# Output projections of a two-layer decoder trunk: operand sums on VectorE, ScalarE and VectorE in a written order

## The chip, the core and the metric

One Trainium2 chip, of which the kernel uses one core. TensorE multiplies matrices, VectorE and GpSimd work element by element, ScalarE evaluates functions and copies, and the queue of SyncE issues all DMAs. The metric is the device time of one execution, in microseconds (us).

## What is computed

Two layers act on a residual stream `x` of 1024 tokens by 1024 features. Cut to what matters here:

```python
for layer in range(2):
    if layer == 0:
        ...                      # ya: gated linear recurrence, yb: sliding-window attention
        y = concat([ya * silu(ga), yb * silu(gb)])    # 1024 x 2048
        x = x + y @ w_out_a[0]                        # w_out_a: 2048 x 1024
    else:
        ...                      # h = rms_norm(x); u, v, g from h @ w_in_c; gated by chunks
        y = u * sg * silu(g)                          # 1024 x 2048
        x = x + y @ w_out_c[0]                        # w_out_c: 2048 x 1024
```

The change lies in the two products `y @ w_out`, the output projections. They are called projection A (layer 0) and projection C (layer 1) below.

## The kernel before

**Splitting.** Every float32 operand of a matrix product is split into a high part (a copy rounded to the fp32r type by ScalarE) and a low part (the difference, by VectorE). `mm3` (L144 to L147) makes a product of three matmuls: high times high, high times low, low times high. `split_a` (L685 to L689) splits a piece of the left operand into a tile named `wa`, `split_b` (L692 to L696) a piece of the right operand into tiles `wh_w` and `wl_w`. The low parts are thus L689 and L696 on VectorE, the high parts L688 and L695 on ScalarE. A piece is 128 x 1024 elements.

**Seven products for eight.** `winograd` (L706) makes a projection by quarters: both operands are cut into quarters, and seven products of sums of quarters take the place of eight. The contraction of 2048 is done as two halves, so there are 14 products, numbered 0 to 13 here (`turns`), and each contains 48 matmuls of 128 x 512: two operand pieces (its halves `j` = 0 and 1), four token tiles, two depths, three matmuls. Each needs a left operand (two `wa` pieces) and a right one (two `wh_w`/`wl_w` pieces). `wa3_0` is the left piece of product 3, half 0.

**The sums.** `sums_a` (L753) makes the sums of the left quarters (`s1` to `s4`): 16 operations of 128 x 1024 for each projection, on GpSimd through `combine` (L748). They are issued in front of products 1, 2, 3, 4, 5 and 7 (table `early`): 2, 4, 2, 4, 2 and 2 operations. The differences of the right quarters (`t1` to `t4`) are 16 more, on VectorE; `sources` issues both pieces of one (L748) ahead of the splitting of the first piece.

**Banks.** The products add up in two sets of four PSUM banks, one bank for each token tile. When the second half of the contraction is through, VectorE adds the four banks to the residual's rows `x1` (L824, called the eviction). It follows products 1, 3, 5, 8, 9, 11 and 13. Product 4 starts afresh in the four banks that products 2 and 3 filled, so its first matmul waits for the eviction after product 3. In projection A, `x1_done` then stores finished rows to `x1dram` and norms them for layer 1 (ScalarE squares with a sum, VectorE scales, GpSimd takes the power -0.5, VectorE multiplies); TensorE transposes normed rows during products 12 and 13.

**Buffers.** Quarters of `w_out` that are still to be used wait in four tiles (`braw`), loaded by SyncE's queue; a load waits until VectorE has read what was there. `wa` pieces have four tiles, `wh_w` and `wl_w` five each. `wa` of product s+1 can thus be written when product s-1 has been through the same half.

**Order.** A scheduler orders each engine's instructions, apart from engines under `manual_schedule`, which run in the order of the code. TensorE is under it throughout. The loop of `winograd` adds GpSimd and SyncE. ScalarE and VectorE are placed by the scheduler there. In the loop, the sums named in `early` for product s come first, then the operands of product s+1, then the matmuls of product s with their evictions. `sources` and `operands` start like this:

```python
            if i == 2:
                combine(nc.vector, t[n], b[n, "b12"], t[n], sub)
                return xs[n], t[n]
...
        def operands(s):
            load_b(s + 1)
            src_a, src_b = sources(*turns[s])
```

## Time and profile before

| | us |
|---|---|
| median of three runs | 1453.38 (1451.16 to 1453.53) |
| span of the profiled execution, first to last instruction | 1451.4 |
| TensorE busy | 1348.5 (93%) |
| VectorE busy | 1111.1 (77%) |
| ScalarE busy | 693.9 (48%) |
| GpSimd busy | 506.3 (35%) |
| chain that ended last, by engine | TensorE 59%, VectorE 22%, waiting for nothing that shows ("issue") 8%, GpSimd 4%, ScalarE 4%, DMA 3% |

The span is the time of one execution inside the profiler; the three runs were timed apart from it, and their median stands 2.0 us above the span. The page gives busy shares over the whole span, which mix stages with different limits, so the stages of the two projections (about 522 to 711 us and 1284 to 1448 us) have to be read from views of those stretches.

### The profile page before, as it was taken

To read this page: it belongs to the slowest core of one execution; us is meant where nothing else is said; L and a number is where in the kernel's file an instruction comes from. 1 tells how busy PE (TensorE), PEld (TensorE's weight loads), DVE (VectorE), ACT (ScalarE), POOL (GpSimd) and SP (SyncE) were. 2 spreads that over 40 slices of the span, in tenths; PEclk is the share of its full clock that TensorE was granted. 3 is DMA by queue.
4 is the path that set the end of the run, shared out by engine and by line. 5 is a ranking of instruction groups with operands and counts; after the bars stand their busy time and mean duration, and the time that the engine had idled before them with its cause. 6 is when DMAs were issued, how large, how long until landed. Compare 5 with 4: busy or idle time off the path is not lost.

```text
span 1451.4 us, 18932 instructions
## 1 busy us (share of the span) xinstructions
PE 1348.5 (93%) x7003; PEld 1148.9 (79%) x7003; DVE 1111.1 (77%) x1830; ACT 693.9 (48%) x1282; POOL 506.3 (35%) x350
## 2 busy tenths in 40 slices
PE   7999999999999996599998799999988998997998
PEld 6888888888887785488888799777777777775887
DVE  6468888888788889778678745778877887879873
ACT  6467878776777763134423223333333333432430
POOL 3322333221032339300035232444455444488100
PEclk9999999999999998799999899999999999999999
DMA  6212111112211054014412123233223322683321
GB/s 208 59 30 58 29 46 30 44 32 71 58 33 51 4 188 174 16 44 146 159 37 80 68 93 135 65 113 113 91 65 117 109 91 66 216 334 132 113 96 64
DMA packets 100536, 133.53 MB, mean 92 GB/s; under 512 B 5355, under 2 KB 72028, under 8 KB 98396
## 3 DMA queue, kind: packets, MB, share of 16 engines
q1 hardware_dynamic: 100444, 132.32, 27.1%
q8 instruction: 55, 0.90, 0.3%
q14 instruction: 37, 0.30, 0.1%
HBM read 107.11 MB, written 25.19 MB: 91 GB/s over the span
## 4 chain that ended last, share of the span: by engine, by line
PE 59%; DVE 22%; issue 8%; POOL 4%; ACT 4%; DMA 3%; SPq 0%; DVEq 0%; POOLq 0%; ACTq 0%
PE m L145 6%; PE m L146 5%; PE m L147 5%; DVE wlg L1142 3%; PE v L145 3%; PE v L146 3%; PE v L147 3%; DVE wl_w L696 2%; DVE wa L689 2%; PE pq L145 2%; PE gb L145 2%; PE pq L147 2%; PE gb L147 2%; PE pq L146 2%; PE gb L146 2%
## 5 line engine op out<-in xcount | busy, mean ns | idle before, releaser
L145 PE MATMUL m<-wh_w,wa 128*128 128x512 f32 x432 | 170.8, 395 | 34.0 <-DVE x L824 34.0
L146 PE MATMUL m<-wl_w,wa 128*128 128x512 f32 x432 | 170.5, 395 | 4.2 <-DVE wl_w L696 4.2
L147 PE MATMUL m<-wh_w,wa 128*128 128x512 f32 x432 | 170.0, 393 | 0.0
L145 PEld LDWEIGHTS m<-wh_w,wa 128*128 128x128 f32 x432 | 82.3, 190 | 52.9 <-issue 32.8
L146 PEld LDWEIGHTS m<-wl_w,wa 128*128 128x128 f32 x432 | 82.3, 190 | 21.6 <-DVE wl_w L696 5.0
L147 PEld LDWEIGHTS m<-wh_w,wa 128*128 128x128 f32 x432 | 82.3, 190 | 17.3
L1226 ACT CAST vh<-vg 128x256 fp32r<-128x256 f32 x64 | 26.0, 407 | 122.3 <-DVE vg L1224 122.3
L530 DVE CUSTOM_DVE_ANT_0 e<-ps,e,sink_bc 128x256 f32<-128x256 f32 (+1 forms) x128 | 62.3, 525 | 20.6 <-PE ps L527 20.2
L600 POOL TENSOR_TENSOR yb<-ot,yb 128x256 f32<-128x256 f32 x32 | 23.6, 736 | 144.9 <-DVE ot L598 127.2
L134 DVE TENSOR_TENSOR wl<-raw,wh 128x1024 fp32r<-128x1024 f32 x38 | 49.4, 1307 | 26.4 <-ACT wh L133 26.2
L1295 POOL TENSOR_TENSOR ug<-yt,ug 128x512 f32<-128x512 f32 x32 | 41.9, 1319 | 71.5 <-DVE yt L1294 71.4
L696 DVE TENSOR_TENSOR wl_w<-b,wh_w 128x1024 fp32r<-128x1024 f32 x36 | 60.7, 1693 | 6.8 <-ACT wh_w L695 6.8
L545 ACT ACTIVATE e<-e,nm 128x256 f32<-128x256 f32 (+1 forms) x128 | 61.6, 486 | 0.4 <-DVE nm L535 0.4
L695 ACT CAST wh_w<-b 128x1024 fp32r<-128x1024 f32 x36 | 37.5, 1046 | 46.9 <-DVE b L748 22.7
L1272 POOL TENSOR_TENSOR ug<-ug,sg 128x512 f32<-128x512 f32 x24 | 40.7, 1699 | 51.0 <-DVE ug L1271 51.0
L824 DVE TENSOR_TENSOR x<-m,x 128x512 f32<-128x512 f32 x56 | 37.4, 684 | 24.9 <-PE m L147 24.7
L902 POOL TENSOR_TENSOR ya<-ya,r 128x1024 f32<-128x1024 f32 x8 | 22.9, 2859 | 91.2 <-DVE r L898 65.5
L145 PE MATMUL pq<-hh,wh 128*128 128x512 f32 x128 | 52.5, 410 | 0.0
L145 PE MATMUL ga<-hh,wh 128*128 128x512 f32 x128 | 50.3, 393 | 2.2 <-DVE ya L867 2.2
L145 PE MATMUL gb<-hh,wh 128*128 128x512 f32 x128 | 50.3, 393 | 0.0
L145 PE MATMUL za<-hh,wh 128*128 128x512 f32 x128 | 50.2, 392 | 0.0
L147 PE MATMUL pq<-hh,wl 128*128 128x512 f32 x128 | 50.2, 392 | 0.0
(405 smaller groups left out, 4619.0 us busy)
## 6 DMA issues: line engine op xcount, KB each, us to landing
raw<-in_w_in_a_dram SPq DMA_DIRECT2D x34, 512.0 KB, 4.1
b<-in_w_out_a_dram SPq DMA_DIRECT2D x22, 512.0 KB, 6.9
b<-in_w_out_c_dram SPq DMA_DIRECT2D x22, 512.0 KB, 6.0
rawg<-in_w_in_c_dram SPq DMA_DIRECT2D x16, 512.0 KB, 3.6
rawu<-in_w_in_c_dram SPq DMA_DIRECT2D x16, 512.0 KB, 3.7
vg<-vdram SPq DMA_DIRECT2D x8, 1024.0 KB, 5.8
ydram<-ug SPq DMA_DIRECT2D x32, 256.0 KB, 2.4
yg<-ydram SPq DMA_DIRECT2D x8, 1024.0 KB, 10.8
```

Source lines behind the costliest of these rows:

```text
L134: nc.vector.tensor_tensor(out=lo, in0=raws[j], in1=hi.bitcast(F32), op=ALU.subtract)
L145: nc.tensor.matmul(acc, lhsT=lh, rhs=rh, start=first, stop=False, skip_group_check=shared)
L146: nc.tensor.matmul(acc, lhsT=lh, rhs=rl, start=False, stop=False, skip_group_check=shared)
L147: nc.tensor.matmul(acc, lhsT=ll, rhs=rh, start=False, stop=last, skip_group_check=shared)
L530: nc.vector.tensor_tensor_reduce(out=e[:, h, k0:256], in0=acc[:, j * 256:j * 256 + kw], in1=e[:, h, k0:256], scale=rs[:, 2 * (b % 4) + j:2 ...
L545: nc.scalar.activation(out=e[:, h], in_=e[:, h], func=AF.Exp, bias=st["nm"][:, h:h + 1], accum_out=st["sums"][:, h:h + 1])
L695: nc.scalar.copy(out=hi, in_=src)
L696: nc.vector.tensor_tensor(out=lo, in0=src, in1=hi.bitcast(F32), op=ALU.subtract)
L824: nc.vector.tensor_tensor(out=dst, in0=accs[m], in1=dst, op=add)
L1142: nc.vector.tensor_tensor(out=lo[:, j], in0=src, in1=hi[:, j].bitcast(F32), op=ALU.subtract)
L1272: nc.gpsimd.tensor_tensor(out=us[j], in0=us[j], in1=gates[j], op=ALU.mult)
L1295: nc.gpsimd.tensor_tensor(out=ug, in0=y.rearrange("p c t -> p (c t)"), in1=ug, op=ALU.mult)
```

## The change

In both projections:

- The 16 sums of the left operand run on VectorE.
- ScalarE and VectorE are also under `manual_schedule` in the loop, so they take their instructions in the order of the code.
- In the loop, the operands of product s+1 are issued first, then the sums that `early` names for product s, then the matmuls and evictions of product s.
- A difference of the right quarters is issued by halves: first piece of it, split of `wa` half 0, split of `w` half 0, then the second piece and half 1. Its line in the new file is L797.
- In projection A the norm of finished rows is cut into its steps, which are issued one and two token tiles later (`norms_step`), the last ones by `finish` after the loop.

The core of the diff:

```diff
+        def norms_step(least):
+        for one in norms:
+            one[0] += 1
+            if one[0] > least and len(one) > 1:
+                one.pop(1)()
...
             if i == 1:
-                combine(nc.gpsimd, xs[n], a21, a22, add)
+                combine(nc.vector, xs[n], a21, a22, add)
             elif i == 2:
-                combine(nc.gpsimd, a21, a11, a21, sub)
-                combine(nc.gpsimd, a11, xs[n], a11, sub)
+                combine(nc.vector, a21, a11, a21, sub)
+                combine(nc.vector, a11, xs[n], a11, sub)
             else:
-                combine(nc.gpsimd, a12, a12, a11, sub)
+                combine(nc.vector, a12, a12, a11, sub)
...
             if i == 2:
-                combine(nc.vector, t[n], b[n, "b12"], t[n], sub)
-                return xs[n], t[n]
+                return xs[n], t[n], (b[n, "b12"], t[n])
...
-            src_a, src_b = sources(*turns[s])
+            src_a, src_b, of = sources(*turns[s])
             pa, pb = [], []
             for j in range(2):
+                if of:
+                    nc.vector.tensor_tensor(out=src_b[j], in0=of[0][j], in1=of[1][j], op=sub)
...
-        manual = tc.manual_schedule(engines={ET.Pool, ET.SP})
+        manual = tc.manual_schedule(engines={ET.Activation, ET.DVE, ET.Pool, ET.SP})
...
+            nxt = operands(s + 1) if s + 1 < count else None
             for args in early.get(s, []):
                 sums_a(*args)
-            nxt = operands(s + 1) if s + 1 < count else None
...
+        finish()
         manual.__exit__(None, None, None)
...
-            _, rs = norm_rs(xt, f"c{t}", late["po"])
-            norm_mul(xt, xt, rs, late["gain_c"])
+            ss = norm_square(xt, f"c{t}", late["po"])[1]
+            rs = []
+            norms.append([0, lambda: rs.append(norm_root(ss, f"c{t}")),
+                          lambda: norm_mul(xt, xt, rs[0], late["gain_c"])])
```

The order of TensorE's instructions stays as it was, and SyncE's changes by one store in the norm's tail. In the rows below, `rawa0` is a right quarter that is turned into a difference in place, `b12_20_0` a quarter just loaded, `m2_0` the first of the four banks of products 2 and 3, and the last number of a name is a buffer's. First VectorE around the end of product 3 of projection A, before:

```order
L689 TENSOR_TENSOR wa4_1_5830<-sa0_1_5666,wa4_1_5830 128x1024
L696 TENSOR_TENSOR wl_w4_1_5834<-rawa1_5500,wh_w4_1_5833 128x1024
L748 TENSOR_TENSOR rawa0_5498<-b22_30_0_5893,rawa0_5498 128x1024
L696 TENSOR_TENSOR wl_w5_0_5903<-b11_0_5591,wh_w5_0_5902 128x1024
L748 TENSOR_TENSOR rawa1_5500<-b22_30_1_5895,rawa1_5500 128x1024
L689 TENSOR_TENSOR wa5_0_5899<-sa1_0_5813,wa5_0_5899 128x1024
L824 TENSOR_TENSOR x1_5570<-m2_0_5761,x1_5570 128x512
L696 TENSOR_TENSOR wl_w5_1_5910<-b11_1_5593,wh_w5_1_5909 128x1024
L824 TENSOR_TENSOR x1_5570<-m2_1_5762,x1_5570 128x512
```

and the same place now:

```order
L755 TENSOR_TENSOR yb0_472<-sa0_0_5683,yb0_472 128x2x512
L755 TENSOR_TENSOR yb1_1030<-sa0_1_5684,yb1_1030 128x2x512
L797 TENSOR_TENSOR rawa0_5498<-b12_20_0_5739,rawa0_5498 128x1024
L696 TENSOR_TENSOR wa4_0_5818<-sa0_0_5683,wa4_0_5818 128x1024
L703 TENSOR_TENSOR wl_w4_0_5822<-rawa0_5498,wh_w4_0_5821 128x1024
L797 TENSOR_TENSOR rawa1_5500<-b12_20_1_5741,rawa1_5500 128x1024
L696 TENSOR_TENSOR wa4_1_5826<-sa0_1_5684,wa4_1_5826 128x1024
L703 TENSOR_TENSOR wl_w4_1_5830<-rawa1_5500,wh_w4_1_5829 128x1024
L755 TENSOR_TENSOR sa1_0_5833<-ya0_4518,ya2_5091 128x1024
L755 TENSOR_TENSOR sa1_1_5834<-ya1_4754,ya3_5453 128x1024
L830 TENSOR_TENSOR x1_5570<-m2_0_5761,x1_5570 128x512
L830 TENSOR_TENSOR x1_5570<-m2_1_5762,x1_5570 128x512
```

Work on the operands of products 5 and 6 stood ahead of the eviction of `m2_0`; now only the operands of product 4 and two sums do, and sums stand among the operands.

Second, VectorE in the last spatial products of layer 1, just before projection C. `yt` adds the banks `s7`, which projection C's first product takes over; `first_c`, `wa0` and `wl_w0` are operands of product 0, `wa1` and `wl_w1` of product 1. Before:

```order
L1271 TENSOR_TENSOR ug7_3_11283<-u7_0_11284,ug7_3_11283 128x512
L696 TENSOR_TENSOR wl_w1_0_11537<-b11c_11493,wh_w1_0_11536 128x1024
L1271 TENSOR_TENSOR ug7_1_11281<-u7_2_11286,ug7_1_11281 128x512
L689 TENSOR_TENSOR wa0_1_11518<-yg1_11488,wa0_1_11518 128x1024
L696 TENSOR_TENSOR wl_w1_1_11544<-b11c_11493,wh_w1_1_11543 128x1024
L1268 TENSOR_TENSOR ug7_2_11282<-u7_0_11284,sg7_11076 128x512
L689 TENSOR_TENSOR wa1_0_11533<-yg4_11496,wa1_0_11533 128x1024
L1292 TENSOR_TENSOR yt7_0_0_11415<-s7_0_0_0_11416,sb7_11070 128x256
L1292 TENSOR_TENSOR yt7_0_0_11415<-s7_0_0_1_11421,sb7_11070 128x256
L689 TENSOR_TENSOR wa1_1_11540<-yg5_11498,wa1_1_11540 128x1024
L1294 TENSOR_TENSOR yt7_0_0_11415<-s7_0_0_0_11416,yt7_0_0_11415 128x256
```

and now:

```order
L696 TENSOR_TENSOR wa0_1_11518<-yg1_11488,wa0_1_11518 128x1024
L1290 TENSOR_TENSOR ug7_1_11281<-u7_2_11286,ug7_1_11281 128x512
L703 TENSOR_TENSOR wl_w0_1_11522<-rawc1_11486,wh_w0_1_11521 128x1024
L696 TENSOR_TENSOR wa1_0_11533<-yg4_11496,wa1_0_11533 128x1024
L1287 TENSOR_TENSOR ug7_2_11282<-u7_0_11284,sg7_11076 128x512
L703 TENSOR_TENSOR wl_w1_0_11537<-b11c_11493,wh_w1_0_11536 128x1024
L1311 TENSOR_TENSOR yt7_0_0_11415<-s7_0_0_0_11416,sb7_11070 128x256
L1311 TENSOR_TENSOR yt7_0_0_11415<-s7_0_0_1_11421,sb7_11070 128x256
L696 TENSOR_TENSOR wa1_1_11540<-yg5_11498,wa1_1_11540 128x1024
L703 TENSOR_TENSOR wl_w1_1_11544<-b11c_11493,wh_w1_1_11543 128x1024
L1313 TENSOR_TENSOR yt7_0_0_11415<-s7_0_0_0_11416,yt7_0_0_11415 128x256
```

`wl_w0_1`, which stood some 25 instructions earlier, now stands between `wa0_1` and the first sum that frees a bank (before, at L1294), and `wa0_1` comes ahead of the `wl_w1` pieces instead of between them.

Third, GpSimd from the end of mixer A on, before:

```order
L902 TENSOR_TENSOR ya3_5453<-ya3_5453,r7_5466 128x1024
L748 TENSOR_TENSOR sa0_0_5665<-yb0_472,yb2_1826 128x1024
L748 TENSOR_TENSOR sa0_1_5666<-yb1_1030,yb3_2677 128x1024
L748 TENSOR_TENSOR yb0_472<-yb0_472 128x2x512
L748 TENSOR_TENSOR yb1_1030<-yb1_1030 128x2x512
L748 TENSOR_TENSOR yb0_472<-sa0_0_5665,yb0_472 128x2x512
```

and now:

```order
L900 TENSOR_TENSOR it7_5467<-it7_5467,xa7_5354 128x1024
L909 TENSOR_TENSOR ya3_5453<-ya3_5453,r7_5466 128x1024
L163 TENSOR_TENSOR nrsc0_6305<-nmc0_6306,half_neg_81 128x1
L163 TENSOR_TENSOR nrsc1_6321<-nmc1_6322,half_neg_81 128x1
L163 TENSOR_TENSOR nrsc2_6337<-nmc2_6338,half_neg_81 128x1
```

The 16 sums between `ya3` and the powers of the norm are gone from it.

## Rows read from the trace of the kernel before

**Rows 1.** TensorE's waits, 521 to 712 us: us in total, times, longest.

```profile
PE m L145 <- DVE x L824: 24.6, 1, 24.6
PE m L146 <- DVE wl_w L696: 4.2, 2, 2.2
```

**Rows 2.** TensorE's waits, 1277 to 1448 us.

```profile
PE m L145 <- DVE x L824: 9.4, 3, 7.4
PE m L145 <- DVE yt L1294: 2.3, 1, 2.3
```

**Rows 3.** Timeline of TensorE, projection A: start us, us, instruction, [idle before <-releaser].

```profile
521.87 0.41 PE L145 MATMUL m<-wh_w,first_a 128*128 128x512 f32 x1
...
546.18 0.50 PE L146 MATMUL m<-wl_w,wa 128*128 128x512 f32 x1 [2.00 <-DVE wl_w L696]
...
559.53 0.79 PE L146 MATMUL m<-wl_w,wa 128*128 128x512 f32 x1 [2.17 <-DVE wl_w L696]
...
596.61 0.76 PE L145 MATMUL m<-wh_w,wa 128*128 128x512 f32 x1 [24.59 <-DVE x L824]
...
693.69 1.04 PE L196 MATMUL ptc<-ident,x 128*128 128x128 f32 x8
...
710.89 0.39 PE L145 MATMUL v<-wh,gh 128*128 128x512 f32 x1
```

**Rows 4.** Timeline of TensorE, projection C; 34 matmul starts after 1439.69.

```profile
1283.64 0.47 PE L145 MATMUL m<-wh_w,first_c 128*128 128x512 f32 x1 [2.33 <-DVE yt L1294]
...
1439.69 0.39 PE L146 MATMUL m<-wl_w,wa 128*128 128x512 f32 x1
...
1447.40 0.39 PE L147 MATMUL m<-wh_w,wa 128*128 128x512 f32 x1
```

**Rows 5.** Stretches: us, each engine's busy us (count), granted clock, DMA share, GB/s.

```profile
571.90:596.60 24.70, 0.12 (x1) 0.02 (x1) 24.70 (x10) 3.04 (x3) 22.88 (x7) 0.59 0.14 51
596.60:603.00 6.40, 6.39 (x20) 5.17 (x21) 6.40 (x8) 0.00 (x0) 0.00 (x0) 0.70 0.01 3
```

**Rows 6.** Timeline of VectorE, projection A, 564 to 596 us.

```profile
564.98 1.21 DVE L748 TENSOR_TENSOR rawa<-b,rawa 128x1024 f32<-128x1024 f32 x1
566.11 3.42 DVE L748 TENSOR_TENSOR b<-b,b 128x1024 f32<-128x1024 f32 x1
569.46 3.43 DVE L696 TENSOR_TENSOR wl_w<-rawa,wh_w 128x1024 fp32r<-128x1024 f32 x1
...
595.78 0.68 DVE L824 TENSOR_TENSOR x<-m,x 128x512 f32<-128x512 f32 x1
```

**Rows 7.** Timeline of GpSimd in the same stretch.

```profile
558.35 3.35 POOL L748 TENSOR_TENSOR sa<-ya,ya 128x1024 f32<-128x1024 f32 x1
565.20 3.25 POOL L748 TENSOR_TENSOR sa<-ya,ya 128x1024 f32<-128x1024 f32 x1 [3.50 <-DVE wa L689]
...
588.18 6.60 POOL L748 TENSOR_TENSOR ya<-ya,ya 128x1024 f32<-128x1024 f32 x2
```

**Rows 8.** A group of VectorE, 620 to 712 us: xcount, busy us, mean ns, idle before.

```profile
L696 DVE TENSOR_TENSOR wl_w<-b,wh_w 128x1024 fp32r<-128x1024 f32 x11 | 13.3, 1219 | 0.4 <-ACT wh_w L695 0.4
```

**Rows 9.** Timeline of ScalarE: two casts of projection A, two of C.

```profile
548.45 1.05 ACT L695 CAST wh_w<-b 128x1024 fp32r<-128x1024 f32 x1 [3.35 <-DMA b<-in_w_out_a_dram]
549.76 1.05 ACT L695 CAST wh_w<-b 128x1024 fp32r<-128x1024 f32 x1 [0.27 <-DMA b<-in_w_out_a_dram]
...
1274.56 1.06 ACT L688 CAST wa<-yg 128x1024 fp32r<-128x1024 f32 x1 [0.74 <-PE u L146]
...
1308.51 1.05 ACT L688 CAST wa<-yg 128x1024 fp32r<-128x1024 f32 x1 [2.81 <-DMA yg<-ydram]
```

**Rows 10.** Timeline of VectorE just before projection C.

```profile
1262.93 2.14 DVE L696 TENSOR_TENSOR wl_w<-rawc,wh_w 128x1024 fp32r<-128x1024 f32 x1
...
1283.08 0.74 DVE L1294 TENSOR_TENSOR yt<-s,yt 128x256 f32<-128x256 f32 x2
```

**Rows 11.** DMA issues, whole span: count, KB each, median us from issue to landing.

```profile
b<-in_w_out_a_dram SPq DMA_DIRECT2D x22, 512.0 KB, 6.9
```

More of the change, by code (lines that the diff above doesn't have):

```diff
@@ L172, in norm_rs, with norm_root @@
         nc.scalar.activation(out=xs, in_=xt, func=AF.Square, accum_out=ss)
+        return xs, ss
+    def norm_root(ss, t):
         rs = small.tile([P, 1], F32, tag="nrs", name=f"nrs{t}")
         power_rsqrt(rs, (ss, 1.0 / D), 1, f"nm{t}")
-        return xs, rs
+        return rs
+    def norm_rs(xt, t, pool):
+        xs, ss = norm_square(xt, t, pool)
+        return xs, norm_root(ss, t)
     def norm_mul(xt, xs, rs, gain, parts=1):
@@ L707, in raw_quarter, with winograd @@
         return load_quarter(lambda j: rawpool.tile([P, 2, 512], F32, tag="raw", name=f"{name}{j}"), w, r0, nh)
-    def winograd(acc_tiles, pool_of, w, parts, b11, first_a, done, after):
+    def winograd(acc_tiles, pool_of, w, parts, b11, first_a, done, after, finish):
         sub, add = ALU.subtract, ALU.add
@@ L769, in sources @@
             if i == 0:
-                return quarter(n, 0, 0), b11[n]
+                return quarter(n, 0, 0), b11[n], None
             if i == 1:
-                return quarter(n, 1, 0), b[n, "b21"]
+                return quarter(n, 1, 0), b[n, "b21"], None
             if i == 2:
-                combine(nc.vector, t[n], b[n, "b12"], t[n], sub)
-                return xs[n], t[n]
+                return xs[n], t[n], (b[n, "b12"], t[n])
             if i == 3:
-                combine(nc.vector, t[n], b[n, "b22"], t[n], sub)
-                return quarter(n, 0, 0), t[n]
+                return quarter(n, 0, 0), t[n], (b[n, "b22"], t[n])
             if i == 4:
-                return quarter(n, 1, 0), b[n, "b22"]
+                return quarter(n, 1, 0), b[n, "b22"], None
             if i == 5:
-                combine(nc.vector, b[n, "b11"], t[n], b[n, "b11"], sub)
-                return quarter(n, 0, 1), b[n, "b11"]
-            combine(nc.vector, t[n], b[n, "b21"], t[n], sub)
-            return quarter(n, 1, 1), t[n]
+                return quarter(n, 0, 1), b[n, "b11"], (t[n], b[n, "b11"])
+            return quarter(n, 1, 1), t[n], (b[n, "b21"], t[n])
         def operands(s):
             load_b(s + 1)
-            src_a, src_b = sources(*turns[s])
+            src_a, src_b, of = sources(*turns[s])
             pa, pb = [], []
             for j in range(2):
+                if of:
+                    nc.vector.tensor_tensor(out=src_b[j], in0=of[0][j], in1=of[1][j], op=sub)
                 if s == 0 and j == 0:
@@ L981, in x1_done @@
             nc.sync.dma_start(out=x1dram[t * P:(t + 1) * P, :], in_=xt)
-            _, rs = norm_rs(xt, f"c{t}", late["po"])
-            norm_mul(xt, xt, rs, late["gain_c"])
+            ss = norm_square(xt, f"c{t}", late["po"])[1]
+            rs = []
+            norms.append([0, lambda: rs.append(norm_root(ss, f"c{t}")),
+                          lambda: norm_mul(xt, xt, rs[0], late["gain_c"])])
+    norms = []
+    def norms_step(least):
[3 more added lines that the diff above has]
+                one.pop(1)()
     def out_a_after(s, j, m):
+        norms_step(1)
         if s == 0 and j == 0 and m == 0:
@@ L1000, in trunk_kernel @@
     winograd(x1, lambda: late["po"], w_out_a, [(1024, yb.__getitem__), (0, ya.__getitem__)], b11, first, x1_done,
-             out_a_after)
+             out_a_after, lambda: [norms_step(0) for _ in range(2)])
     last_spec[0] = len(specs) - 1
@@ L1355, in out_c_after @@
             load_x1(x1dram, x2)
-    winograd(x2, lambda: sp, w_out_c, [(0, yg.__getitem__), (1024, lambda g: yg[4 + g])], b11, first, store, out_c_after)
+    winograd(x2, lambda: sp, w_out_c, [(0, yg.__getitem__), (1024, lambda g: yg[4 + g])], b11, first, store, out_c_after,
+             lambda: None)
 def distance_onehot():
```

2 lines of the change are left out of this document (1 added, 1 removed).

## The prediction

> **What bounds the kernel now.** I read TensorE's waits in the two stretches of the projections first, then its timeline there, and then what VectorE and GpSimd did while it waited. TensorE is busy 93% of the span, so a gain can only come from the places where it stands or runs slowly.
>
> Projection A begins at 521.87 and the next stage's first matmul at 710.89 [rows 3]: 189.0 us. What it has to do: matmuls in an unbroken run start 7.71 / 34 = 0.227 us apart [rows 4], so a product of 48 takes 10.9 us and 14 take 152.4; four groups of transposes of about 1.04 us (one of them stands in [rows 3]) bring it to 156.5. So 32.5 us are lost. Waits are 24.6 + 4.2 = 28.8 of them [rows 1], and the remaining 3.7 are the clock: the matmul after the 2.17 us wait takes 0.79 instead of 0.39, and from 596.6 to 603.0 the granted clock averages 0.70, which alone costs 0.30 x 6.4 = 1.9 [rows 3, 5]. Projection C runs from 1283.64 to 1447.40 + 0.23 [rows 4]: 164.0 against 152.4, so 11.6 lost, of which 9.4 are waits for the eviction [rows 2] and 2.2 the clock after them. Both together: 44.1 us. The last wait each time is the eviction, VectorE's L824.
>
> Why is VectorE late? From 571.9 to 596.6 it is busy the whole 24.7 us with ten instructions, and GpSimd 22.9 us with seven [rows 5]. The same operation takes 1.21 us at 564.98 and 3.42 at 566.11 [rows 6]. Between the two, at 565.20, GpSimd starts again after 3.50 us of rest [rows 7]. GpSimd's own sums take 3.3 us, and an eviction, which reads one operand from PSUM, stays at 0.68 [rows 6, 7]. After 620 us, with GpSimd almost quiet, the low parts average 1.22 us [rows 8]. Back to back they start 1.14 apart (564.98 to 566.11 [rows 6]), since 0.08 overlaps. So a sum on GpSimd stretches each VectorE operation beside it by about 2.2 us, and the low parts, differences and the eviction behind them pile up until TensorE stands.
>
> **The change part by part.**
>
> *Sums moved.* 16 for each projection leave GpSimd and cost VectorE 16 x 1.14 = 18.2 us. The operations that were stretched come back to 1.14. What VectorE now has to do for a product is: four low parts, in most products two differences, zero to four sums, and an eviction of four (4 x 0.6 back to back) after some. With "during product s" for what is queued while TensorE does product s: during product 2, 4 low parts + 4 sums = 8 x 1.14 = 9.1; during 3, 6 + 2 sums + eviction = 8 x 1.14 + 2.4 = 11.5; during 4, 6 + 4 sums = 11.4; during 5, 11.5; during 7, 8 x 1.14 = 9.1; the others 4.6 to 9.3, with norms about 12 around product 10. Against 10.9 that is 1.7 us too much over products 3 to 5 and then slack. Operands are needed only at the end of the product, so this much is covered by being early; the exception is the eviction ahead of product 4.
>
> *Where the queue stands at product 4 of A.* Product 0 starts at 521.87 as before, so product 4 can start at 521.9 + 4 x 10.9 = 565.5. VectorE now keeps the written order: eviction after product 1, operands of 3, four sums, operands of 4, two sums, eviction after 3. The operands of product 3 wait for a load: ScalarE's cast starts at 548.45 when the data land [rows 9]. I allow 0.5 later, since the last step of mixer A on VectorE comes one low part later and the loads queue behind it. Then: cast until 550.0, low part until 551.2, two more (the second cast follows at 549.76 [rows 9]) until 553.4, four sums until 558.0, operands of 4 with 6 x 1.14 + 0.2 (the cast of each half has to come between a difference and its low part, which leaves about 0.1 a half) until 565.0, two sums until 567.3, first bank evicted at 568.0. TensorE waits 2.5 us at product 4. Bounds: 0 if the load lands as much earlier, 6 if it lands 3.5 us later. A wait of 2.17 was followed by the slow clock, one of 2.00 and one of 2.33 were not [rows 3, 4]; at about half a chance of 1.6 us I add 0.8. Products 5 to 13 then find their operands ready: the eviction ends at 569.7, operands of 5 at 576.8, TensorE needs them at 578.9. A loses 3.3 us instead of 32.5.
>
> *Loads and buffers.* The loads need 6.9 us from issue to landing [rows 11]; each has more than a product (10.9 us) between the low part that frees its buffer and the difference that reads it, so in-order waiting on them costs nothing except at product 3, counted above. If that cover were gone, each late load would stop VectorE and the eviction queued behind it. SyncE's loads are issued in the same order. ScalarE needs four casts of about 1.0 us in 10.9: nothing. The norm's steps go behind evictions and run while products 10 to 13 are multiplied; the rows are not transposed until 693.69 [rows 3], some 14 us later than their finished banks: nothing, and at most 1 us if a store must land before a row may be overwritten.
>
> *The start of C.* `wl_w0_1`, done at 1262.93 for 2.14 us beside GpSimd [rows 10], now comes after `wa0_1`, whose cast starts at 1274.56 when TensorE frees its tile [rows 9]; it stands ahead of the sum at 1283.08 [rows 10], which frees the bank that product 0 waits for at 1283.64 [rows 4]. So product 0 starts later by 1.1 to 2.1, less what VectorE has gained by then because those 2.14 us are gone from 1262.93. I take 0.5, and 0.9 for the chance that TensorE, standing longer there, gets the slow clock: 1.4 together, bounds -1 and +4.
>
> *Product 4 of C.* The last left quarter of product 3 is cast at 1308.51 [rows 9], then by the same steps: low parts until 1311.9, four sums 1316.5, operands of 4 at 1323.5, two sums 1325.8, first bank 1326.5. TensorE gets there at 1283.6 + 0.3 + 4 x 10.9 = 1327.5, and the start's delay moves both. I take 0.3, bounds 0 and 3.
>
> *Sum.* 44.1 - 3.3 - 1.4 - 0.3 = 39.1 us. Against the profiled execution: 1451.4 - 39.1 = 1412.3. The median of the runs stands 2.0 above that span, so I forecast 1453.4 - 39.1 = 1414.3.
>
> The sum goes against a rule, so I weigh it. VectorE is 100% busy exactly where the end is set [rows 5], and the change gives it 32 more operations. The Trainium skill (Perfetto Trace Analysis, Optimizing Scalar/DVE Operations) says that when VectorE is saturated, offloading to ScalarE or even GpSimd may make sense. By that rule alone the change goes the wrong way; the sum by it is the 1489.9 of rival 3. The same section warns that the two engines share a read port, so that moving work between them might not help; the 1.21 against 3.42 us is what decides here.
>
> **The rivals.**
>
> 1. *VectorE becomes the bound in products 3 to 5.* If the written order lets nothing overlap, an operation costs 1.23 (its full length and a little) instead of 1.14: 8 x 1.23 + 2.8 = 12.6, 12.3 and 12.6 against 10.9 make 4.8 more at each projection, and each then has a few us at the slow clock. A loses 3.3 + 4.8 + 2.6 = 10.7, C 1.4 + 4.8 + 1.3 = 7.5: 1453.4 - 44.1 + 18.2 = 1427.5. For it: the margin is thin. Against it: back-to-back rows start 1.14 apart wherever GpSimd rests.
> 2. *The start of C takes back its gain.* The last spatial sums wait behind the operands at full stretch beside GpSimd: 4 instead of 1.4, and 3 at product 4 instead of 0.3: 1414.3 + 5.3 = 1419.6.
> 3. *Slower: VectorE stays as full as it is.* If the stretch came from the place (these tiles, or loads that land there) and not from GpSimd, the 32 sums would come on top: at 1.14 each 1453.4 + 36.5 = 1489.9, and stretched to 3.4 like their neighbours still more (products 2 to 5 hold 34 operations and two evictions of 2.4 against 4 x 10.9 = 43.6 us of matmuls, so 34 x 3.4 + 4.8 - 43.6 = 77 us in each projection: 1453.4 - 44.1 + 154 = 1563). It decides from (43.6 + 22 - 4.8) / 34 = 1.79 us for an operation: there a projection loses the 22 us that it loses now on average. Against it: the jump from 1.21 to 3.42 comes within one microsecond of GpSimd's start, on the same line and shape, and the operations before it ran in the same place. The rule of the Trainium skill named above would give this case's lower time.
> 4. *Better: no new wait.* Both new waits and the clock losses vanish and C starts 1 us earlier: 1453.4 - 45.1 = 1408.3.
>
> **How the numbers follow.** The forecast has 0.70, rival 1 has 0.13, rival 2 has 0.09, rival 3 has 0.03, rival 4 has 0.05. The range goes from 1407 (rival 4 with 1 us to spare) to 1426, which takes in rival 2 and the bounds of product 4 (6 and 3) and of the start (+4) together, 1414.3 + 8.8 = 1423.1, and the nearer part of rival 1. About 0.2%, 2.9 us, is what a measurement can tell here. All cases but the third are faster by far more than that; between them and the third lies little, so faster 0.96, same 0.01, slower 0.03.
>
> **What would show it.** Right: VectorE's 128 x 1024 operations in both projections at 1.21 to 1.23 throughout, sums included; GpSimd idle from the end of mixer A to the first norm; the wait for the eviction at product 4 down from 24.6 and 7.4 to a few us; projection A some 160 us long, C some 153. Wrong: 3 us operations with GpSimd idle (rival 3); waits of TensorE for low parts at products 5 to 7 (rival 1); a wait for `yt` at the start of C of 5 us or more (rival 2); a VectorE that stands idle for loads while TensorE waits for it, which I have priced at nothing after product 3.

## The result and the profile after

| | before | after |
|---|---|---|
| median of the runs, us | 1453.45 (1451.16 to 1454.42, four runs) | 1415.03 (1414.49 to 1415.83, four runs) |
| span of the profiled execution, us | 1451.4 | 1412.7 |
| projection A, first matmul to the next stage's first, us | 189.0 | 160.1 |
| from there to projection C's first matmul, us | 572.8 | 574.0 |
| projection C, first to last matmul, us | 164.0 | 155.0 |

The ratio is 0.9744 (95% interval 0.9731 to 0.9758), 38.4 us less. The page of the changed kernel (busy time, share of the span, instructions):

```profile
PE 1346.6 (95%) x7003; PEld 1150.1 (81%) x7003; DVE 1094.0 (77%) x1862; ACT 693.7 (49%) x1282; POOL 399.3 (28%) x318
```

VectorE has 32 operations more and is busy 17 us less; GpSimd is busy 107 us less. TensorE's waits of the changed kernel from 515 to 690 us (first line) and the longest from 1230 to 1412 us (second), which answer to [rows 1, 2]:

```profile
PE m L145 <- DVE x L830: 2.1, 1, 2.1
...
PE m L145 <- DVE yt L1313: 3.8, 1, 3.8
```

The wait of 24.6 us is down to 2.1, the waits inside projection C are gone, and the one at its start has grown from 2.3 to 3.8. TensorE's timeline, as in [rows 3, 4]:

```profile
519.89 0.40 PE L145 MATMUL m<-wh_w,first_a 128*128 128x512 f32 x1
...
565.85 0.47 PE L145 MATMUL m<-wh_w,wa 128*128 128x512 f32 x1 [2.11 <-DVE x L830]
...
679.99 0.39 PE L145 MATMUL v<-wh,gh 128*128 128x512 f32 x1
...
1253.95 0.76 PE L145 MATMUL m<-wh_w,first_c 128*128 128x512 f32 x1 [3.75 <-DVE yt L1313]
...
1408.71 0.39 PE L147 MATMUL m<-wh_w,wa 128*128 128x512 f32 x1
```

VectorE's timeline at the place of [rows 6], and GpSimd's only instruction between 520 and 630 us:

```profile
555.78 1.22 DVE L797 TENSOR_TENSOR rawa<-b,rawa 128x1024 f32<-128x1024 f32 x1
...
562.75 2.35 DVE L755 TENSOR_TENSOR sa<-ya,ya 128x1024 f32<-128x1024 f32 x2
565.02 2.47 DVE L830 TENSOR_TENSOR x<-m,x 128x512 f32<-128x512 f32 x4
567.41 1.21 DVE L797 TENSOR_TENSOR b<-b,b 128x1024 f32<-128x1024 f32 x1
```

```profile
534.34 3.34 POOL L909 TENSOR_TENSOR ya<-ya,r 128x1024 f32<-128x1024 f32 x1 [14.35 <-DVE ya L874]
```

The difference `b<-b,b`, which took 3.42 us, takes 1.21, and the sums, now on VectorE, take 2.35 for two. One stretched operation is left in projection A, beside that last product on GpSimd:

```profile
535.33 3.44 DVE L703 TENSOR_TENSOR wl_w<-b,wh_w 128x1024 fp32r<-128x1024 f32 x1
```

### The profile page after: what moved, and what is told of

The parts are those of the page before. It is cut to its first block, busy times and chain, and to the rows that moved or that the text cites. A ratio compares the mean times of both kernels' runs of the same rounds, so it can differ in the third digit from the quotient of the medians.

```text
span 1412.7 us, 18904 instructions
## 1 busy us (share of the span) xinstructions
PE 1346.6 (95%) x7003; PEld 1150.1 (81%) x7003; DVE 1094.0 (77%) x1862; ACT 693.7 (49%) x1282; POOL 399.3 (28%) x318
## 4 chain that ended last, share of the span: by engine, by line
PE 68%; DVE 16%; issue 6%; POOL 5%; ACT 3%; DMA 2%; SPq 0%; DVEq 0%; POOLq 0%; ACTq 0%
PE m L145 6%; PE m L147 6%; PE m L146 6%; DVE wlg L1161 3%; PE v L145 3%; PE v L147 3%; PE v L146 3%; PE pq L145 2%; PE gb L145 2%; PE pq L147 2%; PE gb L147 2%; PE pq L146 2%; PE gb L146 2%; PE ppt L572 2%; DVE vg L1243 2%
## 5 line engine op out<-in xcount | busy, mean ns | idle before, releaser
L703 DVE TENSOR_TENSOR wl_w<-b,wh_w 128x1024 fp32r<-128x1024 f32 x36 | 46.2, 1284 | 7.8 <-ACT wh_w L702 7.6
L147 PE MATMUL gb<-hh,wl 128*128 128x512 f32 x128 | 49.9, 390 | 0.0
```

The lines of the kernel that those rows point to most:

```text
L147: nc.tensor.matmul(acc, lhsT=ll, rhs=rh, start=False, stop=last, skip_group_check=shared)
L703: nc.vector.tensor_tensor(out=lo, in0=src, in1=hi.bitcast(F32), op=ALU.subtract)
```

## Experiments

All ratios are to the kernel before on the same chip.

### The two halves of the change apart

```diff
 kernel before:                                    # engine alone
-                combine(nc.gpsimd, xs[n], a21, a22, add)      (and the three like it)
+                combine(nc.vector, xs[n], a21, a22, add)
 changed kernel:                                   # order alone
-                combine(nc.vector, xs[n], a21, a22, add)      (and the three like it)
+                combine(nc.gpsimd, xs[n], a21, a22, add)
```

> The kernel before with one edit: the 16 sums of each projection are issued to VectorE; the scheduler still places ScalarE and VectorE, sums stand ahead of the next operands, differences are issued in pairs, norms whole. Theory G (a sum on GpSimd stretches each VectorE operation beside it from 1.14 to about 3.4 us): the stretch goes with the engine alone, so most of the gain is here. VectorE's 128 x 1024 operations in both projections are at 1.2; the wait for the eviction at product 4 of A falls from 24.6 to some 3 to 10 us, since operands of products 5 and 6 (4 to 6 operations of 1.14) may still stand ahead of it; total about 1420, from 1414 to 1430. Rival O (the written order is what pays, the engine is second): the operands ahead of the eviction keep most of the wait, 1440 or more.

Measured: 1420.88 us, ratio 0.9784 (0.9768 to 0.9800). TensorE's waits from 515 to 715 us, and VectorE's timeline ahead of the first of them:

```profile
PE m L146 <- DVE wl_w L696: 5.4, 1, 5.4
PE m L145 <- DVE x L824: 2.2, 2, 1.2
```

```profile
547.14 1.22 DVE L748 TENSOR_TENSOR yb<-sa,yb 128x1024 f32<-128x1024 f32 x1
548.27 1.22 DVE L696 TENSOR_TENSOR wl_w<-b,wh_w 128x1024 fp32r<-128x1024 f32 x1
```

The stretch went with the engine, and the total came out as the first theory had it. But the wait that is left is at another place than expected: the scheduler put seven sums ahead of an operand of product 2, so TensorE waited 5.4 us there, and only 2.2, in two waits, for the eviction.

> The changed kernel with one edit: the 16 sums of each projection go back to GpSimd; written order, differences by halves and norms by steps stay. Theory G: VectorE has 22 operations in products 2 to 5 (22 x 1.14 + two evictions of 2.4 = 29.9 us) and 12 sums on GpSimd beside them stretch some 12 of them by 2.2: 56.3 us against 43.6 of matmuls, so about 12.7 us are lost in each projection, with the slow clock after it some 3: 1415 + 31 - 4 (losses that it replaces) = 1442, from 1428 to 1465; 128 x 1024 operations of VectorE at 3.4 us in both. Rival O: the written order keeps the evictions in time, 1415 to 1422.

Measured: 1428.64 us, ratio 0.9842 (0.9827 to 0.9856). The wait for the eviction in A, and VectorE around it, with GpSimd beside it:

```profile
PE m L145 <- DVE x L830: 8.6, 1, 8.6
```

```profile
568.71 3.37 DVE L696 TENSOR_TENSOR wa<-sa,wa 128x1024 fp32r<-128x1024 f32 x1
572.00 3.36 DVE L703 TENSOR_TENSOR wl_w<-rawa,wh_w 128x1024 fp32r<-128x1024 f32 x1
575.28 2.47 DVE L830 TENSOR_TENSOR x<-m,x 128x512 f32<-128x512 f32 x4
```

```profile
567.66 6.62 POOL L755 TENSOR_TENSOR ya<-ya 128x1024 f32<-128x1024 f32 x2
```

The stretch is back, as in [rows 6]. Yet the time is 13 us under the estimate, at the lower end of its range, and 24 us under the kernel before. In written order the eviction runs right behind the operands of product 4, where in the kernel before it stood behind work on products 5 and 6. A wait of 24.6 becomes 8.6 by that alone: with the sums still on GpSimd, 16 of the 24.6 us were the order (six operations of products 5 and 6 stood ahead of the eviction, at some 3.3 us each, of which not all showed as wait). Lost time in projection A (its length less the 156.5 of work): 32.5 before, 14.3 with the order alone, 10.6 with the engine alone, 3.6 with both. In C: 11.6, 6.8, 1.6, 2.6. **Each half gives most of the gain by itself, and the gains overlap**: 31.4 us for the engine alone and 23.7 for the order alone (1452.3, the kernel before on that chip, less 1420.9 and 1428.6), 38.4 together. Once the engine is changed, the order thus adds some 7 us and not 23.7. Neither rival holds in its pure form.

### GpSimd kept busy beside the moved sums

Three kernels add work to the changed one in `winograd`'s loop, into a scratch tile that nothing reads, each by one of the three statements in the inner loop:

```diff
             for args in early.get(s, []):
                 sums_a(*args)
+                for x in range(4 if args[1] != 2 else 8):
+                    wh = nxt[1][x // 2 % 2][0].bitcast(F32)[:, x % 2, :]
+                    nc.gpsimd.tensor_tensor(out=scratch, in0=wh, in1=wh, op=add)     # kept busy
+                    nc.gpsimd.tensor_scalar(out=scratch, in0=wh, scalar1=1.0,        # one input
+                                            scalar2=None, op0=add)
+                    nc.gpsimd.memset(scratch, 0.0)                                   # writes only
```

> The changed kernel with work added that computes nothing of the result: where a pair of sums is issued on VectorE, GpSimd also adds pieces of the high parts just cast to themselves, into a scratch tile that nobody reads (128 x 512, 64 of them in each projection, 1.30 us each where nothing runs beside them, so as many bytes as the sums had). VectorE has the same instructions on the same tiles. Theory G: VectorE's 128 x 1024 operations beside them go from 1.21 to about 3.4 us; the 24 pieces that fall to products 2 to 5 are worth 12 sums, 12 x 2.2 = 26 us on a VectorE that has 43.6 us of work there against 43.6 of matmuls; with the clock 1415 + 2 x 26 = 1467, from 1440 to 1485. Rival P (the stretch comes from the place, the tiles or the loads that land there): VectorE stays at 1.21 and the total at 1415.

> The changed kernel with work added that computes nothing of the result: the same 64 pieces of 128 x 512 in each projection as with GpSimd kept busy (1444.2 measured), but each adds a constant to the piece, so it reads one operand from SBUF where that one read two. If a VectorE operation with two operands in SBUF and a GpSimd operation that reads SBUF take turns as wholes (2.06 for a VectorE operation between pieces of 1.98 there, 3.4 between sums of 3.3), it makes no difference how many operands GpSimd reads: VectorE's operations beside the pieces last 1.14 plus the piece's own time, and the total lies between 1430 and 1460. If GpSimd's second operand is what costs, VectorE stays at 1.21 and the total at 1415.

> The changed kernel with work added that computes nothing of the result: in the places of the 64 pieces GpSimd fills the scratch tile with zeros, so it reads nothing from SBUF; with nothing to wait for, these run in a row from the end of mixer A on, and from the last spatial product on. If only GpSimd's reading makes the two take turns, VectorE's operations beside the fills stay at 1.21 and the total at 1415, within 1.5. If anything that GpSimd does in SBUF makes them take turns, operations beside the fills are longer by a fill each, and 16 to 32 of them in products 0 to 3 of each projection make the evictions late: 1425 or more.

Measured: 1444.23 us (ratio 0.9948, 0.9933 to 0.9963), 1427.50 us (0.9838, 0.9818 to 0.9858) and 1416.88 us (0.9765, 0.9745 to 0.9784). Each projection has 32 pieces (the last row below), 64 in both; the first two expectations give 64 to each. VectorE and GpSimd in the three, in this order, at the same operands:

```profile
553.50 2.06 DVE L703 TENSOR_TENSOR wl_w<-b,wh_w 128x1024 fp32r<-128x1024 f32 x1
555.48 4.03 DVE L755 TENSOR_TENSOR yb<-yb 128x1024 f32<-128x1024 f32 x2
```

```profile
550.48 15.87 POOL L818 TENSOR_TENSOR scratch<-wh_w 128x512 f32<-128x512 f32 x8 [4.99 <-ACT wh_w L702]
```

```profile
554.02 1.65 DVE L703 TENSOR_TENSOR wl_w<-b,wh_w 128x1024 fp32r<-128x1024 f32 x1
555.59 3.23 DVE L755 TENSOR_TENSOR yb<-yb 128x1024 f32<-128x1024 f32 x2
```

```profile
551.44 16.62 POOL L818 TENSOR_SCALAR scratch<-wh_w 128x512 f32<-128x512 f32 x10 [6.65 <-ACT wh_w L702]
```

```profile
552.86 1.22 DVE L703 TENSOR_TENSOR wl_w<-b,wh_w 128x1024 fp32r<-128x1024 f32 x1
554.00 2.35 DVE L755 TENSOR_TENSOR yb<-yb 128x1024 f32<-128x1024 f32 x2
```

```profile
538.09 18.66 POOL L818 MEMSET scratch<- 128x512 f32 x32
```

Same instructions of VectorE, same tiles, same place: 1.22 us beside fills, 1.65 beside pieces that read one operand, 2.06 beside pieces that read two, and 3.4 beside the sums of twice their size [rows 6]. So the cause is GpSimd, and what counts is that it reads SBUF; the place is out. Beside the eight pieces of the first kernel's row eight operations of VectorE are stretched, and ten beside the ten of the second, so the two engines take turns. VectorE's operations start 3.28 to 3.35 apart beside sums ([rows 6] and order alone), 1.98 (553.50 to 555.48) beside two-operand pieces and 1.57 (554.02 to 555.59) beside one-operand pieces. Less their own 1.14, GpSimd's turn costs about 2.2, 0.84 and 0.43. The fills cost no operation anything.

TensorE's wait for the eviction at product 4 of A in the three, 2.1 us in the changed kernel:

```profile
PE m L145 <- DVE x L834: 14.8, 1, 14.8
PE m L145 <- DVE x L834: 10.8, 1, 10.8
PE m L145 <- DVE x L834: 4.4, 1, 4.4
```

The turns account for it. Ahead of that eviction 16 operations of VectorE stand beside pieces, and VectorE stands for the load of product 3, which lands at another time in each kernel (0.28, 2.80 and 3.29 us of idle time ahead of the low part, against 0.99 in the changed kernel): 2.1 + 16 x 0.84 - 0.7 = 14.8, 2.1 + 16 x 0.43 + 1.8 = 10.8, and 2.1 + 2.3 = 4.4. That load is also why the total with fills is 1.9 above the changed kernel, beyond what I allowed.

Both totals with reading came out low: 1444.2 against an estimate of 1467, at the low end of a range of 1440 to 1485, and 1427.5 below a range of 1430 to 1460. The first expectation took a piece's turn for half a sum's, 1.1 us, the second for the piece's whole duration; measured are 0.84 and 0.43. With 0.84 a piece the first estimate would still be 1415 + 2 x 24 x 0.84 = 1455: it also counted as lost time all the pieces of products 2 to 5, and behind product 4 VectorE has slack, which hides most of them (TensorE waits 2.0 us more in A).

The load of product 3 took 9.2 to 12.4 us from issue to cast in the fourteen profiles, and why was not settled. Of the kernels that have the changed kernel's operations ahead of product 4, unstretched, VectorE stood for that load 0.99 us in the changed kernel, 1.70 in the early split, 2.46 with pairs, 3.29 with fills and 3.77 with the norm whole (early split, pairs and norm whole follow below). TensorE's wait at product 4 is 2.1 in the changed kernel, 1.7 in the early split, whose A starts later, and 3.4, 4.4 and 4.9 in the others.

### The order inside the loop

```diff
+            if s != 3:                                  # sums first
+                for args in early.get(s, []):
+                    sums_a(*args)
             nxt = operands(s + 1) if s + 1 < count else None
-            for args in early.get(s, []):
-                sums_a(*args)
+            if s == 3:                                  # sums around: this stands
+                sums_a(*early[3][0])                    # behind the matmuls of product 3
```

> The changed kernel with one edit: the sums named for products 1, 2, 4, 5 and 7 are issued ahead of the next operands, as before the change; those of product 3 stay behind, because their second tile takes the place of one that the operands of product 4 read. Theory G (the engine is what pays): VectorE has the same work, the four sums of product 2 fill the 0.99 us in which it waits for a load and push the operands of product 3 back by some 3.5, the eviction ahead of product 4 comes at most 1 us earlier: 1415, from 1412 to 1420. Rival O: operands that come 4.6 us later make TensorE wait at products 3, 5 and 6 in both projections, 1422 or more.

> The changed kernel with the sums moved inside the loop: those of products 1, 2, 4, 5 and 7 ahead of the next operands (1411.7 measured so, with a wait of 1.2 us left for the eviction ahead of product 4 of A), those of product 3 behind the matmuls and the eviction of product 3. The eviction then has two sums (2.3 us) less ahead of it. Theory G: no wait at product 4 of A, total 1410.5, from 1408 to 1412.5. Rival: the operands of product 5, which read these sums, come 2.3 us later and TensorE waits for them instead, 1412 or more.

Measured: 1411.70 us (ratio 0.9722, 0.9707 to 0.9736) and 1410.66 us (0.9705, 0.9692 to 0.9718). With the sums first, the wait of 2.1 is 1.2. VectorE makes the four sums of product 2 while the load of product 3 lands, takes up the operands of product 3 at 550.79, after their cast has started at 548.98, and does not stand for the load at all:

```profile
PE m L145 <- DVE x L833: 1.2, 1, 1.2
```

That 1.2 is not followed by slow matmuls, and projection A takes 157.6 us. With the sums around, TensorE has no wait in A, and it takes 156.4, which is all its work (156.5). Instead the eviction now waits for TensorE (2.66 for four in place of 2.47):

```profile
562.77 2.66 DVE L831 TENSOR_TENSOR x<-m,x 128x512 f32<-128x512 f32 x4
```

So the order that the change chose cost about 4 us at this place (160.1 less 156.4 in A); no operand came too late.

```diff
-            for j in range(2):
-                if of:
-                    nc.vector.tensor_tensor(out=src_b[j], in0=of[0][j], in1=of[1][j], op=sub)
+            if of:                                      # pairs
+                combine(nc.vector, src_b, *of, sub)
+            for j in range(2):
...
-            ss = norm_square(xt, f"c{t}", late["po"])[1]
-            norms.append([0, ..., ...])
+            _, rs = norm_rs(xt, f"c{t}", late["po"])    # norm whole
+            norm_mul(xt, xt, rs, late["gain_c"])
```

> The changed kernel with one edit: both pieces of a right difference are issued ahead of the splits, as before the change, not by halves. Theory S (in this order VectorE's sum of work decides, not the place of a difference): operands of a product are six operations of 1.14 either way, so the eviction ahead of product 4 comes when it comes and only the first half of an operand is ready 1.14 later: 1415, from 1413 to 1418. Rival H (TensorE gets to each product just as its first half is ready): it waits up to 1.1 at each of products 5 to 11 of both projections, with clock losses 1420 or more.

> The changed kernel with one edit: in projection A the norm of a finished row tile is issued in one piece behind its eviction, as before the change. VectorE, in written order, then stands for ScalarE's square and GpSimd's power of the same tile ahead of the next eviction: some 3 us for each of four tiles after product 9, 12 us in all, of which products 10 and 11 hide what VectorE has to spare there (10.9 - 6.9 for each). Theory N (the steps are needed because of the written order): TensorE waits some 2 to 6 us at products 10 to 12 or at the end of A, 1418, from 1415 to 1424. Rival: the slack takes all of it, 1415.

Measured: pairs 1417.57 us, ratio 0.9752 (0.9739 to 0.9764), not to be told apart from the change's. The operands of product 4 took VectorE 6.81 us against 6.97 by halves, and TensorE waited nowhere for a second half; its wait of 3.4 us at product 4 is the load's (2.46 us of VectorE's time). Norm whole: 1432.63 us, ratio 0.9846 (0.9829 to 0.9862), some 15 us worse than the estimate and outside its range. VectorE's timeline there:

```profile
633.49 0.68 DVE L830 TENSOR_TENSOR x<-m,x 128x512 f32<-128x512 f32 x1
635.39 0.15 DVE L162 TENSOR_SCALAR nmc<-nssc 128x1 f32<-128x1 f32 x1 [1.22 <-ACT nxsc L171]
636.91 1.28 DVE L188 SCALAR_TENSOR_TENSOR x<-x,nrsc,gain_c 128x1024 f32<-128x1024 f32 x1 [1.36 <-DMA x1dram<-x]
638.11 0.69 DVE L830 TENSOR_TENSOR x<-m,x 128x512 f32<-128x512 f32 x1
```

Each tile costs 4.6 us (633.49 to 638.11), two waits included: 1.22 for ScalarE's square, and 1.36 that ended when the row's store to `x1dram` had landed, because the norm overwrites the row. GpSimd's power, which the expectation named, had ended at 636.19. The queue reached the operands of product 11 at 652.4, and TensorE waited 7.1 us for them and ran at a granted clock of 0.50 until 659.2: some 10 us with what followed. Some 5 more lie behind A (579.2 us from there to projection C, against 574.0). The wait at product 4, 4.9 us with the slow clock behind it, stands ahead of every norm and is the load's; it makes 3.8 us of what this kernel's profile has above the changed one, and the norm's price is the other 15.

No run has the norm by steps without the written order, so what the steps are worth by themselves is not shown. In the written order they are needed: with the norm whole, both halves of the change together (0.9846) are slower than the engine alone (0.9784).

### The start of projection A

```diff
+    ready = [split_b(b11[j], f"w0_{j}") for j in range(2)]
     mix_a_product(7, "ga")
...                                                            # and in winograd, for product 0:
+                pb.append(ready[j] if s == 0 and ready else split_b(src_b[j], f"w{s}_{j}"))
```

> The changed kernel with one edit: both pieces of the right operand of product 0 of projection A are split during the end of mixer A, as before the change; the change puts the second one behind the left piece of product 0. Projection A started 2.0 us earlier with the change, which was not forecast. If the one operation that left mixer A is why, its first matmul is back at 521.3 to 521.9 (519.9 with the change), and VectorE has one operation less in A, so the eviction ahead of product 4 gains 1.1: total 1415.5, from 1414.5 to 1417. Rival: the start of A varies from run to run by that much for another reason and the first matmul stays at 519.8 to 520.8.

Measured: 1413.48 us, ratio 0.9744 (0.9727 to 0.9760), the change's own. The first matmul of A and of product 4, and the end of A:

```profile
521.71 0.40 PE L145 MATMUL m<-wh_w,first_a 128*128 128x512 f32 x1
...
567.23 0.47 PE L145 MATMUL m<-wh_w,wa 128*128 128x512 f32 x1 [1.68 <-DVE x L830]
...
679.74 0.39 PE L145 MATMUL v<-wh,gh 128*128 128x512 f32 x1
```

A starts at 521.71, where it started before the change (521.87). In the three kernels that split both pieces in mixer A it starts from 521.7 to 521.9, in the eleven others from 519.8 to 520.8. So the operation that left mixer A is why A starts earlier, by some 1.6 us; the starts of like kernels differ by up to 1.0 us, and that makes up the rest of the 2.0. A ends at 679.74, no later than the change's 679.99. Of the 1.8 us that the change starts earlier, 0.4 went into its longer wait at product 4 (2.11 against 1.68) and the rest into the slow clock behind that wait, which the early split does not have (granted 1.00 from 567.2 to 571.0).

### The start of projection C

```diff
+                steps.setdefault(1, []).append((head_w, 0))   # in the last group's steps:
+                steps.setdefault(2, []).append((head_a, 0))   # operands of product 0
+                steps.setdefault(4, []).append((head_w, 1))
+                steps.setdefault(6, []).insert(0, (head_a, 1))
...
-    manual.__exit__(None, None, None)                         # one written order from the
...                                                            # last group through projection C
+    for g in (2, 3):                                          # only "loads first":
+        load_y(g)                                             # these ahead of the
+    load_x1(x1dram, x2)                                       # last group's stores
+    for args in spatial:
+        group_spatial(*args)
```

> The kernel with the sums moved around (sums of product 3 behind its eviction, the others first) and the start of projection C written by hand: the operands of product 0 are issued between the steps of the last group, the operands of product 1 behind the last spatial sums, so that no low part stands between the sums that free the banks of product 0. TensorE waited 3.75 us there and ran some 2.5 us at the slow clock after it. Expected if this wait is VectorE's queue: the wait falls to about 1 us and the slow clock goes with it, 5 us less than with the sums moved around alone, about 1405.5, from 1403 to 1409. Rival: the operands of product 1, now behind the sums, or loads behind the stores of the last group come too late for products 1 and 2, and the gain is given back: 1409 or more.

> The version with sums moved around and the start of projection C written by hand (1410.4), with the loads of the third and fourth left pieces and of the residual's rows issued ahead of the last group's stores instead of behind them. There the start of C waited only 0.3, but the loads of the right pieces for product 2 stood on the queue behind those, TensorE waited 1.0 + 0.8 at product 2, and C took 156.6 instead of 154.6. Expected if the queue's order is the cause: no wait at product 2, C at 152.5 to 153.5, total 1407, from 1405.5 to 1408.5. Rival: the bytes and not their order set the landing, 1410 as before this edit.

Measured: 1410.41 us (ratio 0.9705, 0.9692 to 0.9719) and 1406.12 us (0.9691, 0.9677 to 0.9706). In the changed kernel three low parts stood among the sums that free the banks:

```profile
1249.33 1.21 DVE L703 TENSOR_TENSOR wl_w<-b11c,wh_w 128x1024 fp32r<-128x1024 f32 x1
1250.46 0.74 DVE L1311 TENSOR_TENSOR yt<-s,sb 128x256 f32<-128x256 f32 x2
1251.12 1.21 DVE L696 TENSOR_TENSOR wa<-yg,wa 128x1024 fp32r<-128x1024 f32 x1
1252.26 1.21 DVE L703 TENSOR_TENSOR wl_w<-b11c,wh_w 128x1024 fp32r<-128x1024 f32 x1
1253.39 0.74 DVE L1313 TENSOR_TENSOR yt<-s,yt 128x256 f32<-128x256 f32 x2
```

TensorE's waits from 1246 us on in the first of the two kernels, and its start of C in the second:

```profile
PE m L145 <- ACT wh_w L702: 1.0, 1, 1.0
PE m L146 <- DVE wl_w L703: 0.8, 1, 0.8
PE m L145 <- DVE yt L1320: 0.3, 1, 0.3
```

```profile
1247.97 0.47 PE L145 MATMUL m<-wh_w,first_c 128*128 128x512 f32 x1 [0.33 <-DVE yt L1320]
1248.28 0.39 PE L146 MATMUL m<-wl_w,first_c 128*128 128x512 f32 x1
```

The wait of 3.75 went to 0.33 in both, and no slow matmuls follow it. In the first, the gain was given back at product 2, whose loads stood behind others on the queue, as its rival had it: two waits of 0.95 and 0.76 us there, and then a granted clock of 0.50 from 1274.5 to 1277.9. With the loads first, C takes 152.7 us of 152.4, A 156.4 of 156.5. This version is 45.6 us faster than the kernel before and its interval lies below the change's.

## Why the prediction was right

It said 1414.3 us and the median is 1415.0; the span was put at 1412.3 and is 1412.7. By its terms:

- **Projection A.** 3.3 us of loss forecast, 3.6 measured: 2.1 of wait (2.5 forecast) and 1.5 of clock (0.8 forecast, half a chance of 1.6 us, a figure that stands in no row; the slow clock came). The walk through VectorE's queue holds in its steps: six operations for the operands of product 4 in 6.97 us (forecast 7.0), two sums in 2.27, the first bank 0.6 later. Everything lies 2.4 us earlier (565.6 for the 568.0 of the walk), because product 0 started 2.0 us earlier and the load's cast 2.2 (546.74 for 548.95). In the early split, where A starts at the walk's time, product 4 started at 567.23, the wait was 1.68 and A lost 1.5 us in all; with a later load the waits were 3.4 to 4.9, as the walk's bounds (0 to 6, by the load) allow. The mechanism and the place are thus right, and that the loss came out within 0.3 us is luck.
- **Ahead of A.** I wrote "product 0 starts at 521.87 as before" and counted the part that left mixer A only as a delay of the load. It started 2.0 us earlier. VectorE's timeline in mixer A, before and then after the change, shows where:

```profile
480.53 1.23 DVE L696 TENSOR_TENSOR wl_w<-rawa,wh_w 128x1024 fp32r<-128x1024 f32 x1 [2.30 <-ACT wh_w L695]
483.31 1.28 DVE L847 SCALAR_TENSOR_TENSOR xa<-z,cols,xa 128x1023 f32<-128x1023 f32 x1 [1.55 <-ACT xa L845]
```

```profile
481.19 2.60 DVE L854 SCALAR_TENSOR_TENSOR xa<-z,cols,xa 128x1023 f32<-128x1023 f32 x2 [3.41 <-ACT xa L852]
```

  With the low part its cast left too, and the convolution of a channel tile began 2.1 us earlier. The omission cost the forecast nothing: what the early start gained was lost again at product 4 and behind it, as the early split showed.
- **The start of C** is the term that was mis-sized: 1.4 forecast (0.5 of start, 0.9 of clock), 3.8 measured. C's first matmul comes 1.2 us later after the stage before it, and a wait of 3.75 instead of 2.33 was followed by 5.25 us at half the clock, some 2.5 lost. I moved only `wl_w0_1`. That one shows ahead of the last `ug`, for which TensorE now stands 0.81 us (at 1249.46; no such wait before). Between the last `ug` and the sum that frees the bank three low parts of product 1 stand where two stood (1248.73 to 1253.39, 4.66 us, against 4.04 before), and TensorE came to that point 0.8 us earlier after `ug`. It stayed inside the bounds that I gave (-1 to +4).
- **Product 4 of C.** 0.3 forecast, no wait measured.
- **Sum.** 2.4 too little at the start of C and 0.3 in A, against 2.0 ahead of A and 0.3 at product 4 of C: misses of both signs, 0.4 in all. That the total lies within 0.7 us is luck.
- **Loads, ScalarE, norm at nothing.** Right for the change. The norm's price was right only because it is cut into steps: whole, it costs some 15 us.
- **The reason.** "A sum on GpSimd stretches each VectorE operation beside it by about 2.2 us" was shown, with the place excluded. But I summed both halves of the change in one walk and named the stretch as why VectorE is late. The runs show a second cause: with the sums on GpSimd, 16 of the 24.6 us of wait were work for later products that stood ahead of the eviction. The wait is what stands ahead times how long each piece takes, so either cure shrinks what is left for the other. One reading of the rows was wrong, too: the eviction shown at 0.68 us (595.78 [rows 6]) starts after GpSimd's last sum has ended (588.18 + 6.60 = 594.78 [rows 7]) and says nothing of evictions beside sums; other rows do (last section).
- **The rivals.** VectorE as the bound in products 3 to 5: no, its operations start 1.13 to 1.21 apart throughout, and TensorE waits for no low part. The start of C: rival 2's price for it, 4, is what came (3.8), but not by its mechanism, since the low parts among the last sums took 1.21 us each, unstretched, and its 3 us at product 4 of C did not come. The slower case: excluded by the three kernels with GpSimd busy. The rule of the Trainium skill weighed there (Perfetto Trace Analysis, Optimizing Scalar/DVE Operations) pointed the wrong way here: taking the sums off GpSimd made VectorE less busy, 1094.0 us against 1111.1. The case without a new wait: not with this order, but two later orders reached 1410.7 (sums around) and 1406.1 (loads first).

## What to carry to other kernels

Before an operation goes to GpSimd to relieve VectorE, look at what VectorE's two-operand instructions take beside it: here each took its own 1.14 us and GpSimd's turn of 2.2 on top, so the help cost more than it saved. When an eviction is late, count what stands ahead of it in its queue separately from how long each piece takes; here the order alone gave 62% of the gain and the engine alone 82%. In an order written by hand, an operation that waits for another engine or for a store holds up everything behind it, so its steps have to be set apart first (here 4.6 us for a tile of the norm).

## What was unexpected of the hardware

- **Turns, priced by what GpSimd reads.** VectorE's 128 x 1024 operation and GpSimd's instruction alternate, and GpSimd's turn is about 2.2 us for a 128 x 1024 sum, 0.84 for a 128 x 512 piece of two operands, 0.43 for one of one operand and nothing for a fill. Half the size thus cost less than half. The Trainium skill (SBUF — State Buffer, Who interferes with whom) says that a VectorE instruction with two SBUF inputs contends with a GpSimd instruction that reads SBUF and not with one that only writes it; the traces agree, with 1.22 us beside fills against 1.65 and 2.06 beside pieces that read. Evictions, one input of which is in PSUM, keep their 0.6 us each beside sums: in the order alone four took 2.47 us at 575.28 while GpSimd made two sums:
```profile
574.24 5.69 POOL L755 TENSOR_TENSOR ya<-sa,ya 128x1024 f32<-128x1024 f32 x2
```

- **The clock after a wait.** Two stretches of the changed kernel (us, busy us of each engine with counts, granted clock, DMA share, GB/s), the one behind product 4's first matmuls in A and the start of C:

```profile
566.38:569.70 3.32, 3.32 (x9) 2.56 (x8) 3.32 (x4) 1.04 (x2) 0.00 (x0) 0.51 0.03 7
1253.95:1259.20 5.25, 5.25 (x12) 4.09 (x13) 5.12 (x14) 0.00 (x0) 4.63 (x4) 0.50 0.27 102
```

  Granted 0.50 is the lower of the two levels (1.2 of 2.4 GHz). It came after waits of 2.11 and 3.75 us, not after 1.68 (early split), 1.2 (sums first) or 0.33 (loads first), nor after the 2.33 of the kernel before [rows 4]. But it also came after two waits of 0.95 and 0.76 us with one matmul between them (first kernel of the start of C), so the length of a wait does not settle it. The 2.11 us cost 3.6 with the clock and the 3.75 some 6.2, so the last few us here were worth more than they looked.
